# A hybrid attention layer on one core: parts of a key tile queued behind the step's exponential, the gain's scaling on GpSimd, and a new order at the end

## The chip, the cores and the metric

The kernel runs on one core of a Trainium2 chip. The metric is the device time of one execution in microseconds; the median of several executions is compared. A core has five engines that each take their instructions in order: TensorE (PE, matmuls, with its weight loads shown as PEld), VectorE (DVE), ScalarE (ACT), GpSimd (POOL) and SyncE (SP), which issues most of the DMAs. ScalarE and GpSimd issue a few DMAs as well.

## The reference

One layer of a decoder, 512 positions of 1024 channels:

```python
h = rms_norm(x, norm_mix)
q, k, v, u, gate_b, gate_c, g_a, g_b = split(h @ w_in)
# 8 heads of 64, strictly causal
z = q.k / 8
log_fail = where(mask, log_sigmoid(-z), 0)
log_later = reverse_cumsum(log_fail) - log_fail
weights = where(mask, exp(log_sigmoid(z) + log_later), 0)
o_a = weights @ v
y_b = gate_b * causal_conv3(gate_c * u, conv_w)
x += (sigmoid(g_a) * (o_a @ w_a) + sigmoid(g_b) * (y_b @ w_b)) @ w_mix_out
x += softmax_attention(rms_norm(x), rms_norm(mem)) @ w_mem_o    # 4 heads, 256 tokens
gate, up = split(rms_norm(x) @ w_ffn_in)
x += (silu(gate) * up) @ w_ffn_out                              # hidden 2816
return rms_norm(x, norm_final)
```

## The kernel before

**Precision.** Every fp32 operand of a matmul is split into a rounded high tile and a rest: ScalarE casts the high tile, VectorE subtracts it from the source. Three matmuls (high by high, high by low, low by high) stand for one. So each weight tile costs TensorE the product, ScalarE a cast (`wh`, L149) and VectorE a subtraction (`wl`, L150). The pools `wr`, `wh` and `wl` have four buffers each.

**Attention steps (about 30 to 195 us).** There are 16 steps, four head pairs p by four key tiles kt from the last to the first. For a step, `scores` multiplies keys and queries into a bank `z` (L430; four such banks), and ScalarE makes |z|, exp and log of it (L437 to L439). VectorE adds max(z, 0) (L440), which gives e, the negative log of the failures; GpSimd masks it (L395); the high and low tiles `l` of e are made (L409, L410); VectorE adds e of the later keys (L452), and the sum's own split `r` is queued in the list `behind`. `weights` then adds r (L470) and l (L473) times constant matrices into the same bank, ScalarE takes the exponential a (L475), GpSimd masks it, and VectorE makes `ah` and `al` of it (L479, L480). `values` multiplies these with v into o (L492). Between a step's scores and its weights stand projections (`project`, L154 to L156, banks `pr`) for the convolution, for later queries and keys and for gates. `conv` takes three projections per channel tile: c, then u, whose product `cu` VectorE runs through three taps at once (L370 to L374), then b. At the end of a loop turn `settle_behind` issues what is queued, with the step's last weight exponential given as an instruction to stay behind. In this stage the order on each engine is chosen by the scheduler from the program order, the dependencies and such pairs. In turn 9 the factors of the memory's norm go to DRAM and back on GpSimd's queue (`mem_factors`, L526).

**Feed-forward (about 510 to 740).** From here the order on TensorE, ScalarE and VectorE is that of the code (`manual_schedule`). Seven products of half size stand for eight, block (m, i) being product i of hidden tile m, with six weight forms made ahead (`ffn_form`, L832 and L833; sums of weights L822). `reads` copies or adds a product's bank (L864, L866). `residual`, which gives the layer's input, sums the squares of x into `acc` and ends with `squares_mean`, whose split of acc (L184, L185) stands on VectorE; the mean's matmul comes behind block (0, 6).

**The end (about 740 to 851).** `run(i, j, subs)` issues product i of hidden pair j, three matmuls for each half s2, 11 pairs in all. Products 0 to 3 come first, then 4 and 6, with product 5 running along for the first 7 pairs (`BEHIND`). `out_pair` and `out_one` make the weight forms (L991, L924, L1006), `act_third` the forms of products 4 and 5 (f45h, L920). The final gain is loaded and scaled by -0.5 on ScalarE (L1170). `onto` adds a bank to the residual (L1174), `square` sums the squares of a row tile (t, h), `rstd` and `rstd_end` make the row's factor (L1261 to L1280), and `store` scales a tile (L1286 on ScalarE, L1288 on VectorE) and sends it out (L1291). The last four pairs of product 5 come at the very end, the half s2 = 1 of them in two column halves (`last_half`, L1299 and L1303).

```python
for j in (0, 1):
    run(2, j)
    run(3, j)
    part()
...
gain = [f(unit("gain")) for _ in range(2)]
for h in range(2):
    nc.sync.dma_start(gain[h], gfin_d[:, h * 512:(h + 1) * 512].broadcast_to([P, 512]))
    nc.scalar.activation(gain[h], gain[h], AF.Copy, scale=-0.5)
```

Of the kernel before, what the change touches and what calls it, by code (L numbers as in the profile page):

```python
# [13 lines left out]
P = 128  # L14
# [22 lines left out]
LIGHT = 3  # L37
BEHIND = 7

# [4 lines left out]
def hybrid_layer(ctx: ExitStack, tc: tile.TileContext, xT_d, memT_d, mem_d, cols_d, wv_d, win_d,  # L44
# [254 lines left out]

    behind = []  # L300

    def settle_behind(*last):
        while behind:
            behind.pop(0)(*last)

# [48 lines left out]

    yb, held_t = [], [None]

    def conv(c, i):
        if i == 0:
            ps = project(O_GC + c * P)
            gc = held_t[0] = tmp("gc")  # L360
            nc.vector.tensor_tensor(out=gc, in0=ps, in1=r0b, op=ALU.mult)
        elif i == 1:
            ps = project(O_U + c * P)
            gc = held_t[0]
            cu = cpool.tile([P, S + 2], F32, tag="cu", name=nm("cu"), bufs=2)
            nc.gpsimd.memset(cu[:, 0:2], 0.0)
            nc.vector.tensor_tensor(out=cu[:, 2:], in0=ps, in1=r0b, op=ALU.mult)
            nc.vector.tensor_tensor(out=cu[:, 2:], in0=cu[:, 2:], in1=gc, op=ALU.mult)
            t = held_t[0] = tmp("cv")
            nc.vector.tensor_scalar(out=t, in0=cu[:, 2:],  # L370
                                    scalar1=cw[:, 2 * TT + c:2 * TT + c + 1],
                                    scalar2=None, op0=ALU.mult)
            for j in (1, 0):
                nc.vector.scalar_tensor_tensor(out=t, in0=cu[:, j:j + S],  # L374
                                               scalar=cw[:, j * TT + c:j * TT + c + 1],
                                               in1=t, op0=ALU.mult, op1=ALU.add)
# [44 lines left out]
    def scores(p, kt):  # L421
# [11 lines left out]
        for hs, bank in zip(heads_of(kt), zs[p, kt]):  # L433
# [8 lines left out]
            causal(by_head(e, n))  # L442
            bufs = 4 // len(hs)
            sp[p, kt, hs] = lsplit(e, w, f"l{kt}", bufs)
            if kt == TT - 1:
                later[hs] = e
                rest[p, kt - 1, hs] = sp[p, kt, hs]
            elif kt > 0:
                t = by_head(e, n)[:, :, P:]
                before = heads_of(kt + 1)[0] if len(heads_of(kt + 1)) == 1 else hs  # L450
                old = by_head(part_of([later[before]], before, hs, n - P)[0], n - P)
                nc.vector.tensor_tensor(out=t, in0=t, in1=old, op=ALU.add)  # L452
                later[hs] = e
                behind.append(lambda *last, e=e, w=w, hs=hs: rests(p, kt, hs, e, w, last))

# [6 lines left out]
    def weights(p, kt):  # L462
        c0, n = span(kt)
        av[p, kt] = {}
        for hs, bank in zip(heads_of(kt), zs[p, kt]):
# [6 lines left out]
            for part in sp[p, kt, hs]:  # L472
# [6 lines left out]
            nc.vector.tensor_scalar(out=ah, in0=a, scalar1=r, scalar2=None, op0=ALU.mult)  # L479
            nc.vector.scalar_tensor_tensor(out=al, in0=a, scalar=r, in1=f(ah), op0=ALU.mult,  # L480
                                           op1=ALU.subtract)
            for h in hs:
# [58 lines left out]
    g(*args)  # L541
    scores(*steps[0])
    for i in range(len(steps) + 1):
        if i in MEM_AT:
# [129 lines left out]
    def residual(w_dram, act, old, gain, pairs=False):  # L674
# [4 lines left out]
        for m in range(KD):  # L679
# [319 lines left out]
    def one_cast(j):  # L999
# [38 lines left out]
    with tc.manual_schedule(engines={mybir.EngineType.PE, mybir.EngineType.Activation,  # L1038
# [6 lines left out]
        for n, (m, i) in enumerate(uses):  # L1045
# [122 lines left out]
        for h in range(2):  # L1168
            nc.sync.dma_start(gain[h], gfin_d[:, h * 512:(h + 1) * 512].broadcast_to([P, 512]))
            nc.scalar.activation(gain[h], gain[h], AF.Copy, scale=-0.5)  # L1170
        ss = cpool.tile([P, 2 * TT], F32, tag="ss", name="ss")
# [219 lines left out]
```

## Time and profile before

| | us |
|---|---|
| Runs | 852.77, 851.52, 851.42; median 851.52 |
| The profiled execution | 852.91 |
| Its span | 851.2 |
| PE busy | 839.0 |
| DVE busy | 653.0 |
| ACT busy | 455.0 |
| POOL busy | 152.3 |

The profile is of one execution. Its span runs from the first to the last record of the core; the execution's own time is 1.71 us longer. A row of a timeline has the start and the duration in us, the engine, the line of the kernel, the operation, the output and inputs with their sizes, and, in brackets, how long the engine was idle before and what released it. A row of the windows view has the stretch, its length, and for each of PE, PEld, DVE, ACT and POOL the busy time and the count, then the granted clock, the share of the DMA engines and the GB/s they moved. A row of DMA issues ends with the median time from issue to landing.

### The profile page before, as it was taken

The numbers are of one execution on the slowest core, as the hardware profiler recorded it, in microseconds if no ns is written. First come the engines' busy times: TensorE is split into PE (matmuls) and PEld (weight loads), VectorE is DVE, ScalarE is ACT, GpSimd is POOL, SyncE is SP. The second block draws the span as 40 slices with busy tenths as digits, with TensorE's granted clock in tenths as the row PEclk, the third lists the DMA queues.
The fourth block names the chain that finished last, engine by engine and source line by source line (L and its number), as shares of the span: only waits on it lengthen the run. The fifth ranks groups of instructions, "written<-read, shape, count | busy, mean of one in ns | idle before, by whom it ended". The sixth has DMA issues, their size and how long they took to land.

```text
span 851.2 us, 12654 instructions
## 1 busy us (share of the span) xinstructions
PE 839.0 (99%) x4776; PEld 738.2 (87%) x4776; DVE 653.0 (77%) x1036; ACT 455.0 (53%) x808; POOL 152.3 (18%) x163
## 2 busy tenths in 40 slices
PE   9999999999999999999999999999999999999996
PEld 7888887888888899888888889999999999888785
DVE  7768887885766586587455679888888788899786
ACT  7566766574333344444444556655555555576564
POOL 0012121210556640163000101111111110000001
PEclk9999999999999999999999999999999999999999
DMA  8453434225588775566431426677667772465452
GB/s 298 148 154 113 127 97 106 75 77 186 201 303 308 297 247 187 176 228 253 144 79 49 112 75 149 172 183 189 177 190 192 181 185 86 157 219 199 154 186 99
DMA packets 51214, 143.72 MB, mean 169 GB/s; under 512 B 5745, under 2 KB 6769, under 8 KB 48338
## 3 DMA queue, kind: packets, MB, share of 16 engines
q1 hardware_dynamic: 41506, 107.89, 37.5%
q0 software_dynamic: 9360, 34.75, 15.8%
q8 instruction: 37, 0.61, 0.3%
q10 hardware_dynamic: 288, 0.28, 0.1%
q14 instruction: 23, 0.19, 0.1%
HBM read 125.20 MB, written 13.64 MB: 163 GB/s over the span
## 4 chain that ended last, share of the span: by engine, by line
PE 92%; DVE 3%; issue 2%; ACT 1%; DMA 1%; POOL 0%; ACTq 0%; POOLq 0%; DVEq 0%
PE z L843 15%; PE p L1109 10%; PE y L843 7%; PE pr L154 7%; PE pr L155 7%; PE pr L156 7%; PE v L843 4%; PE r L154 3%; PE r L156 3%; PE r L155 3%; PE v L272 3%; PE mq L156 2%; PE mq L154 2%; PE mq L155 2%; PE br L154 2%
## 5 line engine op out<-in xcount | busy, mean ns | idle before, releaser
L149 ACT CAST wh<-wr 128x1024 fp32r<-128x1024 f32 x84 | 88.0, 1051 | 151.3 <-issue 66.0
L150 DVE TENSOR_TENSOR wl<-wr,wh 128x1024 fp32r<-128x1024 f32 x84 | 111.3, 1327 | 37.6 <-ACT wh L149 37.2
L154 PE MATMUL pr<-xgh,wh 128*128 128x512 f32 x288 | 112.8, 392 | 0.0
L155 PE MATMUL pr<-xgl,wh 128*128 128x512 f32 x288 | 112.4, 390 | 0.0
L156 PE MATMUL pr<-xgh,wl 128*128 128x512 f32 x288 | 112.2, 390 | 0.0
L578 POOL TENSOR_TENSOR pre<-pre 128x512 f32<-128x512 f32 x44 | 72.2, 1645 | 30.7 <-DMA pre<-in_w_ffn_out_dram 28.4
L812 POOL DMA_DIRECT2D ws<-in_w_ffn_in_dram x22 | 26.6, 1207 | 257.0 <-DVE wf L833 116.5
L843 PE MATMUL z<-xdh,wf 128*128 128x256 f32 x352 | 70.5, 283 | 0.2 <-ACT sb L864 0.2
L156 PEld LDWEIGHTS pr<-xgh,wl 128*128 128x128 f32 x288 | 54.1, 188 | 11.6
L154 PEld LDWEIGHTS pr<-xgh,wh 128*128 128x128 f32 x288 | 54.1, 188 | 10.7
L155 PEld LDWEIGHTS pr<-xgl,wh 128*128 128x128 f32 x288 | 54.1, 188 | 10.4
L864 ACT COPY sa<-z 128x256 f32<-128x256 f32 x44 | 16.4, 372 | 79.3 <-PE z L843 79.2
L843 PEld LDWEIGHTS z<-xdh,wf 128*128 128x128 f32 x352 | 58.0, 192 | 0.5 <-ACT sb L864 0.4
L833 DVE TENSOR_TENSOR wf<-s,wf 128x512 fp32r<-128x512 f32 x44 | 30.3, 690 | 26.0 <-ACT wf L832 25.8
L843 PE MATMUL z<-xdl,wf 128*128 128x256 f32 x176 | 49.8, 283 | 0.0
L924 DVE TENSOR_TENSOR wl<-wr,wh 128x1024 fp32r<-128x1024 f32 x33 | 40.2, 1218 | 5.0 <-ACT wh L991 4.9
L991 ACT CAST wh<-wr 128x1024 fp32r<-128x1024 f32 x33 | 34.7, 1051 | 6.9 <-DMA wr<-sums 3.0
L843 PE MATMUL z<-xch,wf 128*128 128x256 f32 x176 | 35.4, 284 | 0.1
L843 PE MATMUL y<-xch,wf 128*128 128x256 f32 x176 | 35.4, 283 | 0.0
L843 PE MATMUL v<-xoh,wf 128*128 128x256 f32 x176 | 35.4, 283 | 0.0
L843 PE MATMUL z<-xf,wf 128*128 128x256 f32 x264 | 35.4, 283 | 0.0
L843 PE MATMUL y<-xoh,wf 128*128 128x256 f32 x176 | 35.3, 283 | 0.0
(341 smaller groups left out, 2389.4 us busy)
## 6 DMA issues: line engine op xcount, KB each, us to landing
wr<-in_w_in_dram SPq DMA_DIRECT2D x36, 512.0 KB, 3.4
pre<-in_w_ffn_out_dram POOLq DMA_DIRECT2D x11, 1024.0 KB, 8.2
sums<-pre POOLq DMA_DIRECT2D x11, 1024.0 KB, 5.0
ws<-in_w_ffn_in_dram SPq DMA_DIRECT2D x22, 512.0 KB, 3.7
wg<-in_w_ffn_in_dram SPq DMA_DIRECT2D x22, 512.0 KB, 4.3
ws<-in_w_ffn_in_dram POOLq DMA_DIRECT2D x22, 512.0 KB, 6.0
wr<-sums SPq DMA_DIRECT2D x22, 512.0 KB, 3.8
wr<-in_w_ffn_out_dram SPq DMA_DIRECT2D x16, 512.0 KB, 3.5
```

What stands on the lines that cost most here:

```text
L149: after(nc.scalar.copy(h2, raw), lead[-1:])
L150: lows.append(nc.vector.tensor_tensor(out=l2, in0=raw, in1=f(h2), op=ALU.subtract))
L154: nc.tensor.matmul(ps, a[0], b[0], start=start, stop=False, **kw)
L155: nc.tensor.matmul(ps, a[0], b[1], start=False, stop=False, **kw)
L156: nc.tensor.matmul(ps, a[1], b[0], start=False, stop=stop, **kw)
L578: nc.gpsimd.tensor_tensor(out=t[:, a, :], in0=t[:, a, :], in1=t[:, b, :], op=ALU.add)
L812: nc.gpsimd.dma_start(s13, a[:, 0:4:3, :], accum_op=ALU.add)
L833: nc.vector.tensor_tensor(out=w[:, 1, :], in0=raw, in1=f(w[:, 0, :]), op=ALU.subtract)
L843: nc.tensor.matmul(ps[:, :HS], a, b, start=i < 3 and k == 0 and j == 0, stop=k == KP - 1 and j == 2, skip_group_check=True)
L924: nc.vector.tensor_tensor(out=lo, in0=src, in1=f(hi), op=ALU.subtract)
L991: nc.scalar.copy(hi, raw)
L1109: nc.tensor.matmul(res[i][s2], a[:, ts], b, start=j == 0 and n == 0, stop=n == 2 and j == (BEHIND - 1 if (i, s2) == (5, 1) else NJ - 1))
```

## The change

The attention steps: `scores` no longer splits e at once. Both parts of l and the sum with the later e move to a new function, `fails`, which is queued in a list `urgent` that `settle_behind` empties ahead of `behind`; so these parts come behind the step's weights and values, with ScalarE's cast behind the step's last weight exponential. The taps of the convolution move from `conv`'s second projection to `behind`, with the first of them behind the last `al`. `settle_behind` is called once more after the first step's scores.

The feed-forward's entry: `residual` gives back a function instead of the mean's split, and for the layer's input the split is made behind block (1, 1).

The end: the second halves of product 3 for the first two pairs come behind both first halves. The gain is scaled on GpSimd. Product 5 runs along for 6 pairs instead of 7, so that five stand at the end, and two of its weight tiles come from another pool. The factors, stores and halves of the last row tiles are in a new order.

```diff
-BEHIND = 7
+BEHIND = 6
...
     def settle_behind(*last):
-        while behind:
-            behind.pop(0)(*last)
+        while urgent or behind:
+            (urgent or behind).pop(0)(*last)
...
+    def settle_taps():
+        for c, cu, t in taps:
+            after(nc.vector.tensor_scalar(out=t, in0=cu[:, 2:],
+                                          scalar1=cw[:, 2 * TT + c:2 * TT + c + 1],
+                                          scalar2=None, op0=ALU.mult), als[-1:])
...
+        taps.clear()
...
-            t = held_t[0] = tmp("cv")
...
+            held_t[0] = tmp("cv")
+            taps.append((c, cu, held_t[0]))
+            behind.append(lambda *last: settle_taps())
         else:
+            settle_taps()
             ps = project(O_GB + c * P)
...
-            sp[p, kt, hs] = lsplit(e, w, f"l{kt}", bufs)
...
+            urgent.append(lambda *last, e=e, hs=hs: fails(p, kt, hs, e, n, last))
+
+    def fails(p, kt, hs, e, n, last):
+        w = len(hs) * n
+        sp[p, kt, hs] = lsplit(e, w, f"l{kt}", 4 // len(hs), last)
+        if kt == TT - 1:
+            later[hs] = e
+            rest[p, kt - 1, hs] = sp[p, kt, hs]
+        elif kt > 0:
...
+            nc.vector.tensor_tensor(out=t, in0=t, in1=old, op=ALU.add)
+            later[hs] = e
+            behind.append(lambda *last: rests(p, kt, hs, e, w, last))
...
-            nc.vector.scalar_tensor_tensor(out=al, in0=a, scalar=r, in1=f(ah), op0=ALU.mult,
-                                           op1=ALU.subtract)
+            als.append(nc.vector.scalar_tensor_tensor(out=al, in0=a, scalar=r, in1=f(ah),
+                                                      op0=ALU.mult, op1=ALU.subtract))
...
     scores(*steps[0])
+    settle_behind()
...
-        return xs, xn, squares_mean(acc, TT)
+        return xs, xn, (lambda: squares_mean(acc, TT))
...
+    mean1 = mean1()
...
-        w = wpool.tile([P, 2, 512], F32R, tag=FORM_TAGS[j % 2], name=nm("wq"))
+        pool, tag = (fpool, "wg") if j in (BEHIND, BEHIND + 2) else (wpool, FORM_TAGS[j % 2])
+        w = pool.tile([P, 2, 512], F32R, tag=tag, name=nm("wq"))
...
-            if (m, i) == (0, 6):
+            if (m, i) == (1, 1):
+                mean2 = mean2()
+            elif (m, i) == (0, 6):
...
             run(2, j)
-            run(3, j)
+            run(3, j, [0])
             part()
+        for j in (0, 1):
+            run(3, j, [1])
...
-            nc.scalar.activation(gain[h], gain[h], AF.Copy, scale=-0.5)
+            nc.gpsimd.tensor_scalar(out=gain[h], in0=gain[h], scalar1=-0.5, scalar2=None,
+                                    op0=ALU.mult)
...
         rstd(hi)
+        rstd_end(hi)
+        for t in (2, 3):
+            store(t, 1, "act")
         for j in range(BEHIND, NJ):
             run(5, j, [0])
         onto(ys[0, 1], res[5][0], 0, ys[0, 1], -1)
-        rstd_end(hi)
         square(0, 1)
-        store(2, 1, "act")
+        for t in (2, 3):
+            store(t, 0, "both")
+        rstd(t0)
         half = last_half(0)
-        rstd(t0)
+        rstd_end(t0)
         half()
-        store(2, 0, "both")
-        last_half(1)()
-        rstd_end(t0)
-        store(3, 0, "both")
-        store(3, 1, "act")
+        store(0, 0, "act")
+        half = last_half(1)
+        store(0, 1, "both")
+        half()
         rstd(t1)
-        store(0, 1, "both")
         rstd_end(t1)
-        store(0, 0, "act")
         store(1, 1, "both")
         store(1, 0, "act")
```

How this moves instructions, at three places. The first is ScalarE in the attention steps, around the exponential of step (2, 2) at 140 us: e309_1424 and e312_1435 (now e310_1430) are the two heads of step (2, 1), l and r casts of their splits, wh a weight cast, and a321_1489 (now a317_1476) is the weight exponential of step (2, 2). Before:

```order
L409 CAST l1310_1430<-e309_1424 128x384
L409 CAST l1313_1441<-e312_1435 128x384
L149 CAST wh377_1731<-wr376_1729 128x1024
L475 ACTIVATE a321_1489<-z282_1305 128x512
L409 CAST r1326_1502<-e309_1424 128x384
L437 ACTIVATE e336_1535<-z334_1529 128x512
L437 ACTIVATE e339_1545<-z335_1532 128x512
L409 CAST r1328_1506<-e312_1435 128x384
```

And the same stretch now:

```order
L149 CAST wh375_1726<-wr374_1724 128x1024
L485 ACTIVATE a317_1476<-z282_1305 128x512
L416 CAST l1322_1489<-e309_1424 128x384
L416 CAST l1324_1494<-e310_1430 128x384
L416 CAST r1326_1502<-e309_1424 128x384
L444 ACTIVATE e336_1535<-z334_1529 128x512
L444 ACTIVATE e337_1541<-z335_1532 128x512
L445 ACTIVATE e336_1535<-e336_1535 128x512
L416 CAST r1328_1506<-e310_1430 128x384
```

The two casts of l moved from ahead of the weight cast and the exponential to behind both; the casts of r follow them as before, the second one place later.

The second place is VectorE in the same stretch: cu is the convolution's product, cv its taps, wl a weight's rest, ah and al the parts of the exponential. Before:

```order
L410 TENSOR_TENSOR l1311_1431<-e309_1424,l1310_1430 128x384
L410 TENSOR_TENSOR l1314_1442<-e312_1435,l1313_1441 128x384
L452 TENSOR_TENSOR e309_1424<-e309_1424,e283_1310 128x256
L452 TENSOR_TENSOR e312_1435<-e312_1435,e283_1310 128x256
L367 TENSOR_TENSOR cu319_1477<-pr318_1452,r0b69_363 128x512
L368 TENSOR_TENSOR cu319_1477<-cu319_1477,gc306_1416 128x512
L150 TENSOR_TENSOR wl378_1732<-wr376_1729,wh377_1731 128x1024
L370 TENSOR_SCALAR cv320_1481<-cu319_1477,gcol_119 128x512
L374 SCALAR_TENSOR_TENSOR cv320_1481<-cu319_1477,gcol_119,cv320_1481 128x512
L479 TENSOR_SCALAR ah322_1492<-a321_1489,r071_372 128x512
L374 SCALAR_TENSOR_TENSOR cv320_1481<-cu319_1477,gcol_119,cv320_1481 128x512
L480 SCALAR_TENSOR_TENSOR al323_1493<-a321_1489,r071_372,ah322_1492 128x512
```

And now:

```order
L378 TENSOR_TENSOR cu315_1467<-pr314_1442,r0b69_363 128x512
L379 TENSOR_TENSOR cu315_1467<-cu315_1467,gc306_1416 128x512
L150 TENSOR_TENSOR wl376_1727<-wr374_1724,wh375_1726 128x1024
L489 TENSOR_SCALAR ah318_1479<-a317_1476,r071_372 128x512
L417 TENSOR_TENSOR l1323_1490<-e309_1424,l1322_1489 128x384
L490 SCALAR_TENSOR_TENSOR al319_1480<-a317_1476,r071_372,ah318_1479 128x512
L462 TENSOR_TENSOR e309_1424<-e309_1424,e283_1310 128x256
L417 TENSOR_TENSOR l1325_1495<-e310_1430,l1324_1494 128x384
L359 TENSOR_SCALAR cv316_1471<-cu315_1467,gcol_119 128x512
L462 TENSOR_TENSOR e310_1430<-e310_1430,e283_1310 128x256
L363 SCALAR_TENSOR_TENSOR cv316_1471<-cu315_1467,gcol_119,cv316_1471 128x512
L417 TENSOR_TENSOR r1327_1503<-e309_1424,r1326_1502 128x384
```

The rests of l and the sums of e moved from ahead of cu to behind ah, one rest ahead of al and the others behind it; the taps moved from ahead of ah and al to behind al.

The third place is ScalarE at the end: sq are the sums of squares (over 512 columns, then over the two column halves of the last row tile), the activations of rms the logarithm and exponential of a row's factor, uv and l the scaled tiles that go out. Before:

```order
L1181 ACTIVATE sq1655_8729,ss_8320<-u1561_8294 128x512
L1286 ACTIVATE uv1574_8327<-uv1574_8327,rms_8707 128x512
L1265 ACTIVATE rms_8707<-rms_8707,eps_t_97 128x1
L1266 ACTIVATE rms_8707<-rms_8707 128x1
L1303 ACTIVATE sq1657_8751,ss_8320<-u1562_8296 128x256
L1303 ACTIVATE sq1659_8769,s1b_8708<-u1562_8296 128x256
L1286 ACTIVATE uv1575_8329<-uv1575_8329,rms_8707 128x512
L1265 ACTIVATE rms_8707<-rms_8707,eps_t_97 128x1
L1266 ACTIVATE rms_8707<-rms_8707 128x1
L1286 ACTIVATE l11553_8265<-l11553_8265,rms_8707 128x512
L1286 ACTIVATE l11554_8267<-l11554_8267,rms_8707 128x512
```

And now:

```order
L1304 ACTIVATE uv1574_8327<-uv1574_8327,rms_8701 128x512
L1304 ACTIVATE uv1575_8329<-uv1575_8329,rms_8701 128x512
L1199 ACTIVATE sq1655_8730,ss_8320<-u1561_8294 128x512
L1283 ACTIVATE rms_8701<-rms_8701,eps_t_97 128x1
L1284 ACTIVATE rms_8701<-rms_8701 128x1
L1321 ACTIVATE sq1657_8759,ss_8320<-u1562_8296 128x256
L1304 ACTIVATE l11553_8265<-l11553_8265,rms_8701 128x512
L1321 ACTIVATE sq1659_8782,s1b_8702<-u1562_8296 128x256
L1283 ACTIVATE rms_8701<-rms_8701,eps_t_97 128x1
L1284 ACTIVATE rms_8701<-rms_8701 128x1
L1304 ACTIVATE l11554_8267<-l11554_8267,rms_8701 128x512
```

The scaling of the second uv moved from behind the last square to ahead of row 0's square, and that of the first l from behind the last factor to ahead of the last square; behind the last factor one scaling stands where there were two.

More of the change, by code (lines that the diff above doesn't have):

```diff
@@ L298, in qk_part @@
             settle_behind()
-    behind = []
+    urgent, behind = [], []
     def settle_behind(*last):
-        while behind:
-            behind.pop(0)(*last)
+        while urgent or behind:
+            (urgent or behind).pop(0)(*last)
     def qk_halves(p, i, t, last):
@@ L353, in gate @@
         nc.vector.tensor_tensor(out=t, in0=ps, in1=r0b, op=ALU.mult)
-    yb, held_t = [], [None]
+    yb, held_t, taps, als = [], [None], [], []
+    def settle_taps():
[3 more added lines that the diff above has]
+                                          scalar2=None, op0=ALU.mult), als[-1:])
+            for j in (1, 0):
+                nc.vector.scalar_tensor_tensor(out=t, in0=cu[:, j:j + S],
+                                               scalar=cw[:, j * TT + c:j * TT + c + 1],
+                                               in1=t, op0=ALU.mult, op1=ALU.add)
+        taps.clear()
     def conv(c, i):
@@ L368, in conv @@
             nc.vector.tensor_tensor(out=cu[:, 2:], in0=cu[:, 2:], in1=gc, op=ALU.mult)
-            t = held_t[0] = tmp("cv")
[L370 to L376, printed above, removed]
+            held_t[0] = tmp("cv")
+            taps.append((c, cu, held_t[0]))
+            behind.append(lambda *last: settle_taps())
         else:
+            settle_taps()
             ps = project(O_GB + c * P)
@@ L442, in scores @@
             causal(by_head(e, n))
-            bufs = 4 // len(hs)
-            sp[p, kt, hs] = lsplit(e, w, f"l{kt}", bufs)
[L445 to L454, printed above, removed]
+            urgent.append(lambda *last, e=e, hs=hs: fails(p, kt, hs, e, n, last))
[6 more added lines that the diff above has]
+        elif kt > 0:
+            t = by_head(e, n)[:, :, P:]
+            before = heads_of(kt + 1)[0] if len(heads_of(kt + 1)) == 1 else hs
+            old = by_head(part_of([later[before]], before, hs, n - P)[0], n - P)
+            nc.vector.tensor_tensor(out=t, in0=t, in1=old, op=ALU.add)
+            later[hs] = e
+            behind.append(lambda *last: rests(p, kt, hs, e, w, last))
     def carried(p, kt, hs):
```

## The prediction

> **What bounds the kernel now.** I read the page's first lines, then the windows view by stage, then the timelines of single engines around each place where TensorE stands still, and at the end the table of DMA issues.
>
> ```profile
> span 851.2 us, 12654 instructions
> PE 839.0 (99%) x4776; PEld 738.2 (87%) x4776; DVE 653.0 (77%) x1036; ACT 455.0 (53%) x808; POOL 152.3 (18%) x163
> 30.00:195.00 165.00, 163.62 (x778) 137.98 (x777) 135.25 (x221) 106.14 (x196) 29.75 (x54) 1.00 0.36 112
> 843.00:851.20 8.20, 0.00 (x0) 0.00 (x0) 3.47 (x10) 2.95 (x7) 0.00 (x0) 0.75 0.68 256
> ```
>
> TensorE is busy 839.0 of 851.2 us. The change takes no matmul away, so all that it can win lies in the 12.2 us in which TensorE does nothing: 1.38 us in the attention steps (165.00 less 163.62), 8.20 us after the last matmul, and a few waits that are shown below. The parts of the change go to these places one by one. The profiled execution took 852.91 us, its span and 1.71 around it; the median of the runs is 851.52, which is 1.39 less. I work out what is saved within the span and take it from the median.
>
> **How a wait is priced.** A matmul of 512 columns lasts 0.39 us, but the next one starts 0.23 later (149.23, then 149.46 below): they overlap by 0.16. The idle time that a row shows is counted from the end of the matmul before, so a wait costs that idle time and 0.16 more.
>
> **The attention steps.** The two waits there have one cause.
>
> ```profile
> 130.00 0.57 POOL L526 DMA_DIRECT2D rmb<-rmd  x1 [6.55 <-DMA rmd<-rm]
> ```
>
> ```profile
> 131.03 0.35 DVE L479 TENSOR_SCALAR ah<-a,r 128x256 fp32r<-128x256 f32 x1 [5.35 <-POOL a L395]
> ...
> 139.15 1.03 DVE L410 TENSOR_TENSOR l<-e,l 128x384 fp32r<-128x384 f32 x2 [0.54 <-ACT l L409]
> 140.10 0.75 DVE L452 TENSOR_TENSOR e<-e,e 128x256 f32<-128x256 f32 x2
> ...
> 142.10 1.22 DVE L150 TENSOR_TENSOR wl<-wr,wh 128x1024 fp32r<-128x1024 f32 x1
> ...
> 144.42 0.48 DVE L479 TENSOR_SCALAR ah<-a,r 128x512 fp32r<-128x512 f32 x1
> ...
> 145.47 0.74 DVE L480 SCALAR_TENSOR_TENSOR al<-a,r,ah 128x512 fp32r<-128x512 f32 x1
> ```
>
> ```profile
> 139.44 1.04 ACT L149 CAST wh<-wr 128x1024 fp32r<-128x1024 f32 x1
> 140.39 0.59 ACT L475 ACTIVATE a<-z 128x512 f32<-128x512 f32 x1
> ...
> 142.69 1.15 ACT L438 ACTIVATE e<-e 128x512 f32<-128x512 f32 x2
> ```
>
> ```profile
> 139.06 0.39 PE L155 MATMUL pr<-xgl,wh 128*128 128x512 f32 x1
> ...
> 141.03 0.73 PE L430 MATMUL z<-qk,qk 128*128 128x512 f32 x2 [0.90 <-ACT a L475]
> ...
> 146.27 0.39 PE L492 MATMUL o<-al,v 128*128 128x256 f32 x1 [0.49 <-DVE al L480]
> ...
> 149.23 0.39 PE L156 MATMUL pr<-xgh,wl 128*128 128x512 f32 x1
> 149.46 0.56 PE L430 MATMUL z<-qk,qk 128*128 128x128 f32 x4
> ```
>
> GpSimd's in-order queue holds the reload of the memory's factors (rmb), which waits 6.55 us for a store to land; the mask of a weight tile stands behind it, and VectorE idles 5.35 us for that mask. The backlog reaches TensorE twice: 0.90 + 0.16 at 141.03 and 0.49 + 0.16 at 146.27. The change leaves both of GpSimd's DMAs where they are, so the backlog stays.
>
> The first wait stays whole. The exponential a at 140.39 loses the two casts of l ahead of it but keeps the weight cast wh; that cast needs the buffer which the matmul at 139.06 frees when it ends at 139.45, and it starts at 139.44 already.
>
> The second goes. The l and the sum of e (139.15, 140.10) no longer stand ahead of the conv product and of wl. The product waits for a projection that ends at 139.45, so VectorE's work up to wl comes some 1.2 earlier and wl ends near 142.1. Then ah (0.48), one l (0.51) and al (0.74) stand, and al is there near 143.8 instead of 146.2, ahead of the 145.6 at which TensorE asks for it. The taps, now behind al, feed a product only in a later group.
>
> What is late next: the cast of r on ScalarE waits for the sum of e, now behind al, near 144.15, and queued behind that cast are two magnitudes, two exponentials, two logarithms (a pair of them 1.15), another r cast (0.5), a weight cast (1.04) and only then the next weight exponentials, of 384 columns and 0.5 each. Added up, the first of them ends near 149.5. The score matmuls at 149.46 want its bank and would, with 0.65 won, come up at 148.8: a new wait of 0.7 to 0.75. The stage then gives 0.65 and takes 0.75, **0.1 slower**. Both ends: if the new wait doesn't come and the first goes too, 1.8 won (1.06, 0.65, and some 0.1 of slow restart); if l tiles come late in one or two of these steps, 1.2 lost. In the stage as a whole VectorE is busy 135.25 of 165 us, so the delayed l tiles cost nothing elsewhere as long as that slack covers them; without it, see the slower rival. The early settling after the first step sends q moves to the sync queue ahead of two weight loads, which have time in hand: nothing.
>
> **Feed-forward entry.**
>
> ```profile
> 514.95 0.42 DVE L184 CAST acch<-acc 128x512 fp32r<-128x512 f32 x1
> 515.91 0.69 DVE L185 TENSOR_TENSOR accl<-acc,acch 128x512 fp32r<-128x512 f32 x1
> ```
>
> ```profile
> 519.37 0.62 ACT L832 CAST wf<-s 128x512 fp32r<-128x512 f32 x1 [0.31 <-DVE s L822]
> 519.90 0.36 ACT L864 COPY sb<-z 128x256 f32<-128x256 f32 x1
> ```
>
> ```profile
> 520.32 0.39 PE L843 MATMUL z<-xdh,wf 128*128 128x256 f32 x1 [0.21 <-ACT sb L864]
> ```
>
> TensorE waits at 520.32 for a copy that stands on ScalarE behind a cast, which waits for a sum of VectorE. With the two acc steps gone from ahead of that sum it is up to 1.1 earlier, and the copy no longer late: 0.21 + 0.16, **0.4 won**. The acc steps then run behind the reads of block (1, 1), near 522.5, and their mean's matmul stands behind (0, 6), which is later: covered by two blocks of matmuls.
>
> **The end's first sums.**
>
> ```profile
> 739.82 1.02 PE L1109 MATMUL p<-wh,fh 128*128 128x512 f32 x2
> ```
>
> ```profile
> 739.87 0.42 DVE L891 SCALAR_TENSOR_TENSOR a<-z,fg 128x256 f32<-128x256 f32 x1
> ```
>
> Two matmuls take 1.02 where 0.23 + 0.39 would do: the second writes the bank whose old content VectorE reads until 740.29. With the halves of product 3 in turn that bank is wanted nine matmuls later (2.1 us): **0.4 won**. The forms of product 3 are ready for its first half in both orders, so nothing else of it is late.
>
> **The gain.**
>
> ```profile
> 797.81 0.63 ACT L1170 ACTIVATE gain<-gain 128x512 f32<-128x512 f32 x1 [1.38 <-DMA gain<-in_gain_final_dram]
> 798.35 0.60 ACT L920 CAST f45h<-a 128x512 fp32r<-128x512 f32 x1
> ```
>
> ```profile
> 800.25 1.23 DVE L924 TENSOR_TENSOR wl<-wr,wh 128x1024 fp32r<-128x1024 f32 x1 [0.23 <-ACT wh L991]
> ```
>
> ```profile
> 801.53 0.50 PE L1109 MATMUL p<-wl,f45h 128*128 128x512 f32 x1 [0.56 <-DVE wl L924]
> ```
>
> ScalarE waits 1.38 for a load, multiplies, and only then casts f45h and wh, which wl and TensorE's 801.53 wait for. On GpSimd the multiplication waits apart, the cast starts earlier by the idle and the 0.63 at least, and wl by more than the 0.72 that TensorE waits: with its slow restart (0.50 for 0.39), **0.8 won**. GpSimd's step may slow one VectorE step that runs beside it; VectorE itself waits 0.23 there. Bounds: 0.8, or 0 if the raw weights are the next late thing.
>
> **The end's chain.**
>
> ```profile
> 843.73 0.19 ACT L1303 ACTIVATION_READ_ACCUMULATOR sq<-u 128x1 f32 x1
> ...
> 844.96 0.20 ACT L1266 ACTIVATE rms<-rms 128x1 f32<-128x1 f32 x1
> ```
>
> ```profile
> 843.67 0.74 DVE L1288 SCALAR_TENSOR_TENSOR elh<-elh,rms,gain 128x512 f32<-128x512 f32 x1
> 844.33 0.27 DVE L1261 TENSOR_SCALAR rms<-ss,s1b 128x1 f32<-128x1 f32 x1
> ...
> 845.36 0.27 DVE L1275 TENSOR_SCALAR rms<-rms 128x1 f32<-128x1 f32 x1
> ```
>
> ```profile
> 846.63 0.33 SPq L1291 DMA_DIRECT2D out_dram<-u  x1
> ```
>
> Two steps are held by scalings of older tiles on VectorE: the last sum, at 844.33, though its square was there at 843.92, and the factor at 845.36, though its Exp ended at 845.16. One scaling still stands ahead of the sum, but starts 0.3 sooner, since the factor's steps for row 0 are done before; the second hold-up goes (0.15). On ScalarE the last square now stands behind a scaling and may start 0.07 late. Sum: the last store is issued **0.37 earlier**, less 0.05 for the extra pair below.
>
> **The landing.**
>
> ```profile
> 847.00:849.00 2.00, 0.00 (x0) 0.00 (x0) 0.00 (x0) 0.00 (x0) 0.00 (x0) 0.53 1.00 379
> ```
>
> ```profile
> out_dram<-elh SPq DMA_DIRECT2D x2, 256.0 KB, 2.0
> out_dram<-l ACTq DMA_DIRECT2D x1, 256.0 KB, 3.3
> ```
>
> The six last stores go out within 2 us, keep the DMA engines full (share 1.00 at 379 GB/s), and the last lands 3.3 us after its issue; the earlier elh stores landed in 2.0. With the change only two are left for the end. One alone is 2.0, of which its bytes are 0.69 (256 KB at 379 GB/s); behind one more of that size the last lands in 2.7: **0.6 won**. Bounds: 0 (the 3.3 stays) and 1.3 (the 2.0).
>
> The Trainium skill speaks against this step ("DMA: Bandwidth & Descriptors", section "Anatomy of one DMA — SWDGE (gpsimd) path"): about 2.0 us fixed and the bytes at 436 GB/s, which as an estimate is 2.6 for one store and 3.2 for two, so that 0.1 would be won and the time be 849.6. The section is on GpSimd's path and these stores are on others; the trace's 2.0 for a whole store differs from its 2.6, which is why I take the row.
>
> **The extra pair.** Three matmuls of 512 columns become six of 256. Four of 128 columns hold TensorE 0.56, one of 512 columns 0.39 (149.46, 149.23): 0.06 for each start more. Three more starts cost 0 to 0.17; at 256 columns I take 0.05.
>
> **The sum.** -0.1 + 0.4 + 0.4 + 0.8 + 0.37 + 0.6 - 0.05 = 2.4, so 851.52 - 2.4 = **849.1**.
>
> **The rivals.**
>
> *Both attention waits go* (wh finds its buffer free earlier, and the next weight exponential comes in time): 1.9 more, 847.2. For it: ScalarE is idle over a third of the stage (106.14 busy of 165). Against it: 139.44 and 139.45. 0.12.
>
> *The landing doesn't shorten*: the last two stores land in 3.2 to 3.3 whatever went before; 0.6 less, 849.7. For it: the last stores in the trace all share the engines with others, and no row shows a pair by itself. 0.12.
>
> *The waits only move* (the change doesn't do what it says): the attention stage loses 1 us, or the raw weights hold f45h's product at 801, so that 0.8 to 1.6 of the sum is missing: 849.9 to 850.9. For it: each of these waits has another thing of about the same date behind it. 0.2.
>
> *Late l tiles, slower.* In every attention step with earlier keys, twelve of them, the l split now stands on VectorE and ScalarE behind the step's weights. If it is late by 0.5 us, one VectorE step of 512 columns, in each, TensorE's second z products wait 6 us in the stage: 851.5 + 6 - 2.3 = 855.2. It decides from the point where new waits there exceed 4.1 us. For it: VectorE is 82% busy in the stage and has little room after a late step. Against it: TensorE does two projections between a step's scores and its weights. 0.14.
>
> **How the numbers follow.** About 0.2% (1.7 us) is what a measurement of this kernel can tell from no change: faster is below 849.8, slower above 853.2. The forecast has 0.42. Faster: 0.42, the first rival's 0.12, half of the second (0.06), 0.01 of the third: 0.61. Same: 0.06 and 0.19: 0.25. Slower: 0.14. The forecast's own bounds, with those of landing (0 to 1.3) and attention (-1.2 to 1.8) not both at an end, are 847.8 to 850.2. With the first rival at its near side, and the third, the range is 847.1 to 850.9; what is left out is the slower rival and a little of the first.
>
> **What would show it.** In the profile after: al no longer before TensorE's o, and a score matmul near 149 waiting some 0.7 for a; TensorE idle in that stage within 0.3 of 1.38; no wait at 520.3; no wait of the second product of sum 3; f45h cast near 794 and no wait for wl near 801; last store issued 3.4 after the last matmul and landed in 2.7. The prediction is wrong if TensorE idles over 2.5 us in the attention stage, or if the sum of its waits outside goes down by less than 1.

## The result and the profile after

The changed kernel takes 848.86 us (median of five runs, 847.72 to 849.18) against 851.52; the ratio is 0.9961, with an interval of 0.9950 to 0.9972. The forecast was 849.1. The sum held; one of its steps did not, and a second one had only half of its cause.

The first line of the page of the changed kernel, and its window over the attention steps:

```profile
span 847.2 us, 12667 instructions
```

```profile
30.00:195.00 165.00, 163.94 (x779) 138.40 (x778) 134.33 (x222) 105.55 (x197) 27.90 (x54) 1.00 0.40 113
```

The profiled execution took 848.86, 1.66 more than its span. The span is 4.0 shorter than before, more than the 2.7 of the medians, and 1.1 of that is not of the change. The windows of both kernels from 3.0 to 7.5 us, before and then after, show it:

```profile
3.00:7.50 4.50, 4.50 (x12) 3.18 (x11) 2.54 (x5) 2.51 (x4) 0.00 (x0) 1.00 1.03 326
```

```profile
3.00:7.50 4.50, 4.50 (x17) 3.23 (x16) 2.68 (x5) 2.63 (x5) 0.00 (x0) 1.00 1.00 322
```

TensorE counts as busy all the time in both, yet 12 matmuls stand there in the one execution and 17 in the other: five of 0.23 us, 1.1 us. A row of TensorE of each, before and then after:

```profile
6.85 0.89 PE L272 MATMUL v<-wvl,xgh 128*128 128x512 f32 x2
```

```profile
6.03 1.09 PE L272 MATMUL v<-wvl,xgh 128*128 128x512 f32 x4
```

Two matmuls take 0.89 in the one, four 1.09 in the other. The granted clock of 1.00 in both windows is no evidence against a slower clock: the trace holds no clock record before 7.43 us in the one and before 4.91 in the other, and the view prints 1.00 where there is none. The record that begins at these times says full speed, and within 0.3 us of it, in all 14 traces of this case, a matmul of 512 columns starts every 0.23 us instead of every 0.43. It begins between 4.8 and 7.4 us, in no order with the edits, so this is a difference of executions, and the stages are compared without it.

TensorE is idle 1.06 us in the attention steps instead of 1.38. The rows there, of TensorE, ScalarE and VectorE of the changed kernel:

```profile
135.54 0.27 PE L502 MATMUL o<-al,v 128*128 128x128 f32 x1
135.94 0.50 PE L154 MATMUL pr<-xgh,wh 128*128 128x512 f32 x1
...
138.38 0.39 PE L155 MATMUL pr<-xgl,wh 128*128 128x512 f32 x1
...
138.83 1.07 PE L437 MATMUL z<-qk,qk 128*128 128x512 f32 x4
...
147.95 0.66 PE L437 MATMUL z<-qk,qk 128*128 128x128 f32 x4 [0.93 <-ACT a L485]
```

```profile
137.27 1.04 ACT L149 CAST wh<-wr 128x1024 fp32r<-128x1024 f32 x1
138.21 0.60 ACT L485 ACTIVATE a<-z 128x512 f32<-128x512 f32 x1
138.69 0.93 ACT L416 CAST l<-e 128x384 fp32r<-128x384 f32 x2
142.59 0.51 ACT L416 CAST r<-e 128x384 fp32r<-128x384 f32 x1 [2.96 <-DVE e L462]
...
147.42 0.86 ACT L485 ACTIVATE a<-z 128x384 f32<-128x384 f32 x2
```

```profile
141.47 0.74 DVE L490 SCALAR_TENSOR_TENSOR al<-a,r,ah 128x512 fp32r<-128x512 f32 x1
142.13 0.42 DVE L462 TENSOR_TENSOR e<-e,e 128x256 f32<-128x256 f32 x1
```

The four score matmuls at 138.83 run in one piece, where the third of them waited 1.06 before. al is ready at 142.2 and nothing waits for it. The cast of r waits 2.96 us for the sum of e behind al, and the exponential a at the end of that queue makes the score matmuls at 147.95 wait 0.93, with the overlap 1.09. A second, smaller wait stands at 135.94: 0.13 idle, some 0.3 from start to start. Its row names no releaser.

In the feed-forward's entry and in the end the three waits that the prediction named are gone. The entry and the end's first sums had no run of their own; these two rest on the traces. The rows of the entry, of ScalarE and TensorE:

```profile
517.56 0.62 ACT L844 CAST wf<-s 128x512 fp32r<-128x512 f32 x1 [0.31 <-DVE s L834]
518.09 0.37 ACT L876 COPY sb<-z 128x256 f32<-128x256 f32 x1
```

```profile
518.75 0.28 PE L855 MATMUL z<-xdh,wf 128*128 128x256 f32 x1
```

Of product 3 at the end, two matmuls take 0.61 where they took 1.02:

```profile
740.19 0.61 PE L1124 MATMUL p<-wh,fh 128*128 128x512 f32 x2
```

And behind it: TensorE busy throughout from 790 to 835, ScalarE with its cast of f45h, and GpSimd with the gain, beside it:

```profile
790.00:835.00 45.00, 45.00 (x214) 37.09 (x214) 37.76 (x51) 25.39 (x44) 12.62 (x6) 1.00 0.48 155
```

```profile
793.86 0.62 ACT L932 CAST f45h<-a 128x512 fp32r<-128x512 f32 x1
```

```profile
793.72 6.95 POOL L1187 TENSOR_SCALAR gain<-gain 128x512 f32<-128x512 f32 x2 [96.05 <-PE p L1124]
```

Behind the last matmul, which ends at 839.94, VectorE, that matmul, the last issue on ScalarE's queue, and its line in the table of DMAs:

```profile
840.38 0.74 DVE L1306 SCALAR_TENSOR_TENSOR u<-u,rms,gain 128x512 f32<-128x512 f32 x1
841.04 0.27 DVE L1279 TENSOR_SCALAR rms<-ss,s1b 128x1 f32<-128x1 f32 x1
...
841.91 0.27 DVE L1293 TENSOR_SCALAR rms<-rms 128x1 f32<-128x1 f32 x1 [0.41 <-ACT rms L1284]
```

```profile
839.66 0.28 PE L1317 MATMUL p5b<-wq,f45l 128*128 128x256 f32 x1
```

```profile
843.16 0.37 ACTq L1309 DMA_DIRECT2D out_dram<-l  x1
```

```profile
out_dram<-l ACTq DMA_DIRECT2D x1, 256.0 KB, 2.8
```

The last two stores are issued 3.2 us behind the last matmul (before 3.77), and the last one lands in 2.8 (before 3.3). From the last matmul to the span's end it is 7.2 us instead of 8.35 (the prediction's 8.20 is counted from 843.00, and that matmul ended at 842.85).

### The profile page after: what moved, and what is told of

Read it like the earlier page. It is cut to its first block, busy times and chain, and to the rows that moved or that the text cites. A ratio compares the mean times of both kernels' runs of the same rounds, so it can differ in the third digit from the quotient of the medians.

```text
span 847.2 us, 12667 instructions
## 1 busy us (share of the span) xinstructions
PE 837.0 (99%) x4779; PEld 737.9 (87%) x4779; DVE 654.0 (77%) x1036; ACT 453.3 (54%) x806; POOL 158.9 (19%) x165
## 4 chain that ended last, share of the span: by engine, by line
PE 95%; DVE 2%; ACT 1%; issue 1%; POOL 0%; POOLq 0%; DVEq 0%; ACTq 0%
PE z L855 15%; PE p L1124 12%; PE y L855 7%; PE pr L154 7%; PE pr L155 7%; PE pr L156 7%; PE v L855 4%; PE r L155 3%; PE r L154 3%; PE r L156 3%; PE v L272 3%; PE mq L156 2%; PE mq L154 2%; PE mq L155 2%; PE br L156 2%; PE br L155 2%
## 5 line engine op out<-in xcount | busy, mean ns | idle before, releaser
L150 DVE TENSOR_TENSOR wl<-wr,wh 128x1024 fp32r<-128x1024 f32 x84 | 112.4, 1340 | 36.5 <-ACT wh L149 35.9
L936 DVE TENSOR_TENSOR wl<-wr,wh 128x1024 fp32r<-128x1024 f32 x33 | 41.0, 1243 | 4.7 <-ACT wh L1003 4.7
```

The lines of the kernel that those rows point to most:

```text
L150: lows.append(nc.vector.tensor_tensor(out=l2, in0=raw, in1=f(h2), op=ALU.subtract))
L936: nc.vector.tensor_tensor(out=lo, in0=src, in1=f(hi), op=ALU.subtract)
```

## The experiments

Each was timed in five rounds beside the kernel before, whose medians were 851.45 to 851.83; a median of one kernel moves by some 0.4 between such groups, once by 0.7 (below). So the verdicts rest on the waits in the traces, with the time as a second witness. For the same reason five times lie 0.05 to 0.2 outside the range of a theory that their traces bear out: the attention part alone, the rest alone, the gain back on ScalarE, and the changed kernel with the tie, both times.

**The attention part alone.** The kernel before with this part, the rest untouched:

```diff
+            urgent.append(lambda *last, e=e, hs=hs: fails(p, kt, hs, e, n, last))
...
+            taps.append((c, cu, held_t[0]))
+            behind.append(lambda *last: settle_taps())
...
     scores(*steps[0])
+    settle_behind()
```

> The kernel before with the attention part of the change alone (l parts, sums of e and taps queued, the extra settling). Theory (the attention part gives little, because the wait is moved to a later step): the waits at 140 and 146 us are gone, the score matmuls near 147 to 149 wait about 1.1 us for the weight exponential a, and the time is 0.3 to 0.6 under the kernel before, 850.9 to 851.2. Rival (the attention part carries the gain): 1.5 or more under it, 850.0 or less.

Measured: 851.40 against 851.73, ratio 0.9997 (0.9988 to 1.0006): 0.3 less, which the interval can't tell from nothing. Its trace has one wait in the stage, in the place of two:

```profile
148.27 0.66 PE L437 MATMUL z<-qk,qk 128*128 128x128 f32 x4 [0.81 <-ACT a L485]
```

What follows: in this trace the part replaces 1.06 + 0.65 by 0.97. The theory's wait is there; what it is worth in time stays between nothing and 0.7. The rival, that this part carries the gain, falls.

**The rest alone.** The changed kernel with the attention part put back as it was:

```diff
-            urgent.append(lambda *last, e=e, hs=hs: fails(p, kt, hs, e, n, last))
+            sp[p, kt, hs] = lsplit(e, w, f"l{kt}", bufs)
...
-            taps.append((c, cu, held_t[0]))
-            behind.append(lambda *last: settle_taps())
```

> The changed kernel without the attention part (feed-forward entry, product 3's halves, the gain on GpSimd and the end's order alone). Theory: 0.4 + 0.4 + 0.8 in TensorE's waits and 1.0 behind the last matmul, 2.3 to 2.6 under the kernel before, 848.9 to 849.2, with the waits at 140 and 146 us as before (1.06 and 0.65). Rival (the attention part carries the gain): at most 1 under it, 850.5 or more.

Measured: 849.34 against 851.73, ratio 0.9974 (0.9965 to 0.9983), 2.4 less. TensorE's waits in the attention steps are those of before:

```profile
140.88 0.73 PE L430 MATMUL z<-qk,qk 128*128 128x512 f32 x2 [0.88 <-ACT a L475]
...
146.13 0.39 PE L492 MATMUL o<-al,v 128*128 128x256 f32 x1 [0.50 <-DVE al L480]
```

What follows: the feed-forward and the end carry nearly all of the gain.

**The taps put back.** The changed kernel with the convolution's taps where they stood:

```diff
-            taps.append((c, cu, held_t[0]))
-            behind.append(lambda *last: settle_taps())
+            t = held_t[0] = tmp("cv")
+            nc.vector.tensor_scalar(out=t, in0=cu[:, 2:],
...
```

> The changed kernel with the convolution's taps back where they stood, ahead of al on VectorE. Theory (the taps are what lets al be in time, 1.9 us of VectorE work ahead of it): TensorE waits for al again, 0.3 to 0.5 us near 144, the step after is later too, and the time is 0.3 to 1.0 over the changed kernel, 849.2 to 849.9. Rival (moving l alone does it): the same as the changed kernel within 0.2, 848.7 to 849.1.

Measured: 849.48, 0.6 over the changed kernel's 848.86. The time is inside the theory's range, but the wait is another one. TensorE and VectorE:

```profile
144.98 0.45 PE L476 MATMUL z<-l,negtri 128*128 128x384 f32 x1 [1.13 <-DVE l L410]
```

```profile
141.47 0.48 DVE L370 TENSOR_SCALAR cv<-cu,gcol 128x512 f32<-128x512 f32 x1
141.98 0.75 DVE L374 SCALAR_TENSOR_TENSOR cv<-cu,gcol,cv 128x512 f32<-128x512 f32 x1
142.65 0.48 DVE L482 TENSOR_SCALAR ah<-a,r 128x512 fp32r<-128x512 f32 x1
143.04 0.75 DVE L374 SCALAR_TENSOR_TENSOR cv<-cu,gcol,cv 128x512 f32<-128x512 f32 x1
143.71 0.75 DVE L483 SCALAR_TENSOR_TENSOR al<-a,r,ah 128x512 fp32r<-128x512 f32 x1
144.37 0.56 DVE L410 TENSOR_TENSOR l<-e,l 128x384 fp32r<-128x384 f32 x1
```

With the taps ahead of ah and al, the rest of l, which the change puts behind, is late for TensorE's z product, 1.3 us; the wait for a at the next scores does not come. From the projection that starts at 130.11 to the one at 149.81 TensorE takes 19.70 us, as long as in the kernel before (130.15 to 149.85) and 0.34 more than in the changed kernel (129.09 to 148.45). This is the mechanism of the prediction's slower rival, in one step. So the taps' move is what pays for l's: without it the attention part leaves this stretch as long as it was. The other 0.3 of the 0.6 is not shown to be the taps' (this trace also has the wait near 303 us, told at the end, at its longest).

**The reload later in the program.** The changed kernel, and below it the kernel before, with the reload of the memory's factors written three loop turns later:

```diff
-        rmb = cpool.tile([P, MEM], F32, tag="rmb", name="rmb")
-        nc.gpsimd.dma_start(rmb, d.broadcast_to([P, MEM]))
-        return rm, rmb
+        return rm, d
+
+    def mem_reload(d):
+        rmb = cpool.tile([P, MEM], F32, tag="rmb", name="rmb")
+        nc.gpsimd.dma_start(rmb, d.broadcast_to([P, MEM]))
+        return rmb
...
+        if i == MEAN_AT + 3:
+            rmb = mem_reload(rmd)
```

> The changed kernel with the reload of the memory's factors issued three loop turns later on GpSimd's queue. Theory (the backlog of the masks behind that reload is the one cause of all waits between 130 and 150 us, before and after): VectorE's idle time of 5 us for the mask near 130 goes, and with it the wait of about 1.1 at the score matmuls and of 0.3 at the projection ahead; 1.2 to 1.5 under the changed kernel, 847.4 to 847.7. Rival (the new order on ScalarE makes its own wait): the wait stays, 848.6 to 849.1.

> The kernel before with the reload of the memory's factors three loop turns later and nothing else. Theory (the backlog behind the reload made both waits): the waits of 1.06 and 0.65 at 140 and 146 us go, 1.7 to 1.9 under the kernel before, 849.6 to 849.8. Rival (the order on ScalarE and VectorE makes them): they stay, 851.2 to 851.6.

Measured: 848.87 and 852.33 (against 851.62 for the kernel before, ratio 1.0007, 0.9998 to 1.0015). Both were misses of the edit and not of the theory. GpSimd's row in the first of them:

```profile
129.11 0.57 POOL L539 DMA_DIRECT2D rmb<-rmd  x1 [6.45 <-DMA rmd<-rm]
```

The scheduler put the reload back at its old place in the queue; on all five engines the instructions stand as they did in the changed kernel and in the kernel before. So these two only say how far a repeat of a kernel lies off: 0.0 and 0.7.

**The reload tied behind a mask.** The same, with the reload made to follow the last mask of the step written before it, in the changed kernel and in the kernel before:

```diff
+        masks.append(nc.gpsimd.affine_select(
...
-        nc.gpsimd.dma_start(rmb, d.broadcast_to([P, MEM]))
+        after(nc.gpsimd.dma_start(rmb, d.broadcast_to([P, MEM])), masks[-1:])
```

> The changed kernel with the reload of the memory's factors tied behind a mask three steps later on GpSimd, so that the scheduler can't put it back ahead of the mask of step (2, 3). Theory (the backlog behind that reload is the one cause of all waits between 130 and 150 us): VectorE's idle time of 5 us near 130 and TensorE's waits of 0.3 near 136 and 1.1 near 147 go; 1.2 to 1.5 under the changed kernel, 847.4 to 847.7. Rival (the new order on ScalarE, with the cast of r behind al's sums, makes its own wait): the wait near 147 stays, 848.6 to 849.1.

> The kernel before with the same tie and nothing else. Theory: the waits of 1.06 and 0.65 us at 140 and 146 go, 1.7 to 1.9 under the kernel before, 849.6 to 850.0; the attention part of the change then has nothing left to win. Rival (the order of the l and tap steps makes them): they stay, 851.2 to 851.9.

Measured: 847.29, 1.6 under the changed kernel, ratio to the kernel before 0.9945 (0.9933 to 0.9958); and 849.84 against 851.83, 2.0 less, ratio 0.9977 (0.9968 to 0.9987). GpSimd and the attention window of the first, then the window of the second:

```profile
122.07 0.40 POOL L402 TENSOR_SCALAR_AFFINE_SELECT e<-e 128x256 f32<-128x256 f32 x1 [1.24 <-DVE e L448]
123.25 1.12 POOL L402 TENSOR_SCALAR_AFFINE_SELECT a<-a 128x256 f32<-128x256 f32 x1 [0.79 <-ACT a L486]
...
152.73 0.57 POOL L540 DMA_DIRECT2D rmb<-rmd  x1
```

```profile
30.00:195.00 165.00, 165.00 (x786) 139.66 (x786) 135.73 (x223) 107.49 (x199) 29.05 (x54) 1.00 0.41 118
```

```profile
30.00:195.00 165.00, 165.00 (x787) 139.65 (x786) 136.62 (x222) 107.41 (x198) 29.31 (x54) 1.00 0.37 116
```

In the changed kernel this mask of a ran at 129.66:

```profile
129.66 0.42 POOL L402 TENSOR_SCALAR_AFFINE_SELECT a<-a 128x256 f32<-128x256 f32 x1
```

Now it runs at 123.25, the reload at 152.73 waits for nothing, and TensorE is busy for all 165.00 us in both kernels. What follows: the reload in GpSimd's queue was the one cause of the attention waits, before and after the change. The new order makes no wait of its own.

**The tie without the attention part.** All parts of the change but that one, with the tie, beside the changed kernel with the tie:

The edit to the rest alone:

```diff
+        masks.append(nc.gpsimd.affine_select(
...
+        after(nc.gpsimd.dma_start(rmb, d.broadcast_to([P, MEM])), masks[-1:])
```

> The kernel before with the tie on the reload and all parts of the change but the attention part. Theory (the attention part only dodges the backlog and has nothing to win once the backlog is gone): no wait of TensorE between 30 and 195 us and the same time as the changed kernel with the tie, 847.1 to 847.6. Rival (the attention part wins something by itself): 0.5 or more over that kernel, 847.8 or more.

> The changed kernel with the tie once more, beside the kernel without the attention part. Theory: 847.1 to 847.6, equal to the other within 0.3. Rival: 0.5 or more under the other.

Measured: 847.53 (0.9951, 0.9937 to 0.9964) and 847.65 (0.9952, 0.9939 to 0.9964). They are equal: once the queue is clear, the attention part wins nothing.

**The gain back on ScalarE.** The changed kernel with one edit:

```diff
-            nc.gpsimd.tensor_scalar(out=gain[h], in0=gain[h], scalar1=-0.5, scalar2=None,
-                                    op0=ALU.mult)
+            nc.scalar.activation(gain[h], gain[h], AF.Copy, scale=-0.5)
```

> The changed kernel with the gain's scaling back on ScalarE. Theory: ScalarE waits for the gain's load again, the cast of f45h and wl are late, and TensorE waits about 0.7 near 797: 0.8 over the changed kernel, 849.6 to 849.8. Rival (something else is late there, or the slower VectorE steps beside GpSimd cost as much): within 0.3 of the changed kernel, 848.6 to 849.2.

Measured: 849.86, 1.0 over the changed kernel, and the wait is back. ScalarE, then TensorE:

```profile
795.69 0.63 ACT L1187 ACTIVATE gain<-gain 128x512 f32<-128x512 f32 x1 [1.41 <-DMA gain<-in_gain_final_dram]
796.23 0.60 ACT L932 CAST f45h<-a 128x512 fp32r<-128x512 f32 x1
```

```profile
799.40 0.50 PE L1124 MATMUL p<-wl,f45h 128*128 128x512 f32 x1 [0.45 <-DVE wl L936]
```

0.45 + 0.16 and the slow restart of 0.11 are 0.7 in the trace. The theory holds: this one edit brings the wait, and without it TensorE waits for nothing there.

**The end put back.** The changed kernel with the old number of pairs and the old order of row tiles:

```diff
-BEHIND = 6
+BEHIND = 7
...
-        rstd_end(hi)
-        for t in (2, 3):
-            store(t, 1, "act")
...
```

> The changed kernel with the order of the last row tiles and the number of pairs at the end as they were. Theory (order and landing both count): from the last matmul to the span's end 8.3 instead of 7.3, and the time 1.0 to 1.1 over the changed kernel, 849.8 to 850.0. Rival (the order counts, but the last pair of stores lands in 3.2 whatever went before): 0.4 to 0.6 over it, 849.2 to 849.5.

Measured: 849.49, 0.6 over the changed kernel. Its trace says more: the last matmul ends at 839.99 and the span at 848.2, 8.26 behind it, against 7.2; ScalarE's last store and its landing:

```profile
843.75 0.38 ACTq L1308 DMA_DIRECT2D out_dram<-l  x1
```

```profile
out_dram<-l ACTq DMA_DIRECT2D x1, 256.0 KB, 3.3
```

The last store is issued 3.76 behind the last matmul and lands in 3.3, both as before. By the trace the theory holds (1.04), and the landing, 3.3 here and 2.8 in the changed kernel, speaks against the rival. The time, 849.49, lies inside the rival's range; but the 0.4 that it lacks to the theory is within what a median moves by, so the times don't decide.

**Four pairs, new order.** The changed kernel with one number put back, and the two weight tiles in their old pool:

```diff
-BEHIND = 6
+BEHIND = 7
```

> The changed kernel with four pairs at the end instead of five and the new order kept. Theory (the fifth pair covers VectorE's scalings and factors, 3.4 us of work in the 3.5 us of the halves): with four pairs, 2.8 us, the last eviction is 0.5 to 0.7 late, and the time is 0.4 to 0.7 over the changed kernel, 849.2 to 849.6. Rival (the pair only costs its matmul starts): 0.05 to 0.1 under it, 848.8.

Measured: 849.34, 0.5 over the changed kernel. Its last matmul ends at 839.37. VectorE, ScalarE's last store, and its landing:

```profile
839.65 0.27 DVE L1292 TENSOR_SCALAR rms<-rms 128x1 f32<-128x1 f32 x1
...
840.03 0.48 DVE L1191 SCALAR_TENSOR_TENSOR u<-p5b,nrt,u 128x256 f32<-128x256 f32 x1
```

```profile
843.43 0.38 ACTq L1308 DMA_DIRECT2D out_dram<-l  x1
```

```profile
out_dram<-l ACTq DMA_DIRECT2D x1, 256.0 KB, 2.8
```

The last eviction starts 0.66 behind the last matmul, because VectorE is still at row 0's factor, and the last store is issued 4.06 behind it, 0.84 later than with five pairs. The landing is 2.8 either way, so the landing comes from the order of the stores, and the fifth pair pays by covering VectorE's scalings.

## Why the prediction was right, step by step

*The attention steps* were forecast 0.1 slower and gave 0.3 (TensorE idle 1.06 for 1.38; 0.3 in the time of the part alone, 0.5 between the changed kernel and the rest alone). In the six profiles with the new order and the reload at its old place TensorE idles 0.81 to 1.06 in this stage, in the three with the old order 1.37 to 1.40, so the sign is clear. The failed step is "the first wait stays whole". It rested on the cast wh at 139.44 starting just when a matmul ends at 139.45, which I took for a buffer coming free. In the changed kernel the same cast runs at 137.27, more than a microsecond ahead of that matmul (138.38): the two times met by chance. What held the cast in the kernel before stands ahead of it on ScalarE, the two casts of l, the first of which waits 0.63 for GpSimd's mask:

```profile
138.61 0.93 ACT L409 CAST l<-e 128x384 fp32r<-128x384 f32 x2 [0.63 <-POOL e L395]
```

So the first rival was right that the first wait goes. Its other half, that the new wait doesn't come, was wrong: it came, at 1.09 instead of the 0.7 to 0.75 of the forecast. Counted from the score matmuls near 139, TensorE, not held there, asked for the bank some 1.2 sooner than forecast, and the exponential came only 0.9 sooner. The misses cancel in part: 1.06 won that was not forecast, less 0.35 for the longer new wait and 0.3 for the wait at 135.94. The idle time fell by 0.32, just past the 0.3 that the prediction allowed for. The part's whole ground, a backlog behind the reload, was read rightly; the tie shows it.

*Feed-forward entry* 0.4: the copy now ends 0.3 ahead of the matmul, and no idle time is left. *The end's first sums* 0.4: their rows run at 0.23 a matmul. This gain lay in time that the profile counts as busy (the 1.02 for two matmuls), so not all that could be won was in the 12.2 us of idle time. *The gain* 0.8: 0.7 in the trace of the run that puts it back, 1.0 in its time. As far as the traces show, these three were right in mechanism and size.

*The end's chain*, forecast 0.37 less 0.05, gave 0.5 (3.77 to 3.2 for the last store). The sum of row 1 starts 1.1 behind the last matmul instead of 1.5, and the second hold-up is gone: the factor at 841.91 waits for its Exp. So the two hold-ups were read rightly and the term was 0.2 too small; but the order of the steps, to which it was put down, does not do it alone (the extra pair, below).

*The landing*, forecast 0.6: 3.3 to 2.8, so 0.5. The estimate for a pair from a lone store and the bytes was 2.7. The rule of the Trainium skill that I set against it ("DMA: Bandwidth & Descriptors", section "Anatomy of one DMA — SWDGE (gpsimd) path") gave 3.2 as an estimate for the pair. That section is on GpSimd's path; for these stores the trace has 2.8, and the measurement decides.

*The extra pair* was costed by its starts alone, 0.05. The step that failed here is leaving out what the pair covers: it buys 0.84 in the issue of the last store, which I had put down to the new order in the chain. With the new order and no extra pair the last store is issued later than before the change (4.06 for 3.77).

*Not forecast*: between 300 and 312 us TensorE waits for VectorE, at most once in a trace and at one of two places. Before it was 0.23 at 303.42, with the overlap; after it is 0.50 at 310.76, behind VectorE's steps that run beside GpSimd's adds (304.46 to 309.73) at twice their time:

```profile
306.25 2.32 DVE L150 TENSOR_TENSOR wl<-wr,wh 128x1024 fp32r<-128x1024 f32 x1
308.50 1.78 DVE L174 TENSOR_TENSOR ml<-g,mh 128x512 fp32r<-128x512 f32 x1
```

Over the experiments this wait is anything from 0 to 0.94 with no order in it; why it varies stays open.

Added up, 0.3 + 0.4 + 0.4 + 0.8 + 1.1 behind the last matmul, less 0.3 at 310, are the 2.7 of the medians. That the forecast of 2.4 lies so near is in part luck: 0.4 too little in the attention steps and 0.3 not seen at 310 offset each other.

The slower rival did not happen: in the changed kernel TensorE waits for no l tile. The run with the taps put back has such a wait in one step; the rival needed 4.1 us of them.

## What to carry to other kernels

A wait is best removed at its head. Here one transfer in an in-order queue made VectorE idle 5 us, and reordering what stood downstream moved the wait along, for about 0.3; tying that transfer behind a later step took all of it, 2.0 in the kernel before. That two times coincide in a trace does not show that one waits for the other: look for the instruction ahead of it on its own engine before naming a buffer. And where a scheduler chooses the order, moving a line in the program may move nothing; look at the order that comes out, and tie what must stay behind.

## What the runs showed of the hardware

- At the start TensorE begins a matmul of 512 columns every 0.43 us, and every 0.23 once the trace's record of the granted clock begins, at 4.9 us in one execution and at 7.4 in another. That is 1.1 us between two executions. The windows view prints a clock of 1.00 for the time that has no record; the spacing of the matmuls shows the difference.
- VectorE's subtraction of 128x1024 takes 1.21 us alone (at 310.53 in the changed kernel) and 2.32 beside GpSimd's adds; one of 128x512 takes 0.68 (at 309.56 in the kernel before) and 1.78.
- Of two stores of 256 KB issued within 0.03 us, with no DMA moving from 843.2 to 844.0, the later lands after 2.8 us; the last of a row of six lands after 3.3.
